# A two-layer hybrid encoder on one core: the first products in step over x, shorter lags for the last heads' norm, the FFN's sum of squares behind the second pair

## The chip, the cores and the metric

The kernel runs on one core of a Trainium2 chip. The metric is the device time of one execution in microseconds (us): the median of several runs. A profiled execution gives the trace; its span runs from the first to the last instruction.

## What is computed

A batch of one sequence: x is 512 tokens of 1024 channels, float32. Two layers, each of this form (shortened):

```python
h = rmsnorm(x, norm1_g[l])
u = h @ w_in[l]                       # q, k, v (512 each), GLU input (1024), Fourier input (512)
y_a = (rmsnorm(diff_attention(q, k, v, lam), subln_g[l]) * (1 - lam_init)) @ w_proj_a[l]
g = ga * sigmoid(gb)
cv = layernorm(depthwise_conv31(g, conv_w[l]) + conv_b[l])
y_b = silu(cv) @ w_proj_b[l]
y_c = real(fft2(four_in)) @ w_proj_c[l]
ga, gb, gc = split(sigmoid(h @ w_gate[l] + b_gate[l]))
x = x + (ga * y_a + gb * y_b + gc * y_c) @ w_out[l]
h2 = rmsnorm(x, norm2_g[l])
f_gate, f_up = split(h2 @ w_ffn_in[l])
x = x + (silu(f_gate) * f_up) @ w_ffn_out[l]
```

The attention has 8 heads of two 32-wide components. The FFN is 2816 wide.

## The kernel before

Everything lies with channels on the 128 partitions and the 512 tokens along a row, so x is 8 tiles of 128x512. Every product of float32 matrices is made of three matmuls (`gemm`): both sides are split into a high part (a cast on ACT) and a low part (a subtraction on VectorE, DVE), and high x high, high x low and low x high are summed in a PSUM bank. A weight chunk is 8 tiles of 128x128 for one output tile, 512 KB: `chunk` loads it on SyncE's queue (tile `wr`), casts it on ACT (`wh`, L202) and subtracts on DVE (`wl`, L203). x itself is split into tiles A and B (L158, L159); the normed x is split into X.

PSUM has 8 banks: three "main", two "s", two "att" and one "oth". A product that wants a bank of a tag waits until an earlier content of that tag is read.

The stages of a layer: `glu` makes four pairs of gated tiles from x that is not normed yet and scales the results by the inverse root of the mean square (`inv_rms`: squares on ACT, L386; added on GpSimd, L389; summed over partitions by a matmul with ones, L396; then L397 to L403 on DVE and ACT). In layer 1 the squares of all eight tiles are needed at the second gated pair. Then come q, k, v, the heads, the Fourier branch, the convolution, the gates and the projections of the three branches, `w_out`, and the FFN.

The attention (`heads`) and the convolution (`conv`: its taps on DVE, and at its end a norm over channels with two ones matmuls, L1112 and L1114 behind it) are pieces of work that are put among the products of the other stages. Each is an event with a due time (`later`), and `gemm` runs due events between its steps. `norm(hp)` sums the squares of a pair of heads and works out a scale on DVE, `scale(hp)` spreads it, transposes it and multiplies (L932); then `gemm_two` projects the heads. Their lags are `LAG_N` and `LAG_S`.

The FFN's input product is made in pairs, one gate tile and one up tile each, in a form with seven products of halves in place of eight (`pair_weights`, `pair_gemm`, L317, matmuls of 256 columns). The weights' combinations are made on DVE (L289 to L300) with casts on ACT. Pair u uses both banks of the tag ("s", "att", "main")[u % 3]; so the fourth pair needs the banks of the first. The first pair goes over all but the last of x's combined pieces first, and the last is added at its end, since it comes late. Each pair is evacuated by `unit` (L562 to L571), which needs the norm of this stage, `rb2`. It is asked for between the second pair's matmuls and the first pair's evacuation in the code:

```python
if done + j == 1:
    rb2 = self.inv_rms(acc, D, "ar", "rb")
while held:
    act.append(unit(*held.pop(0)))
```

The order on each engine is not that of the code. A scheduler sorts the instructions by a priority (`at`, in time units of the intended schedule) as their inputs become ready in a simulated timeline; each engine then runs its own queue in that fixed order. `after(ins)` ties an instruction behind the last matmul for the scheduler's order alone.

Of the kernel before, what the change touches and what calls it, by code (L numbers as in the profile page):

```python
# [16 lines left out]
P = 128  # L17
L = 2
D = 1024
# [15 lines left out]
WARM = 12  # L35
# [9 lines left out]
XP = (-100000, -15000, -15000, -15000, -10000, -10000, -10000, -10000)  # L45
SQP = 3000
# [9 lines left out]
LAG_S = 20000  # L56
LN = (6000, 14000, 29000)
# [23 lines left out]
def lam_init(l):  # L81
    return 0.8 - 0.6 * math.exp(-0.3 * l)
# [7 lines left out]
class Hybrid:  # L90
# [292 lines left out]
    def sq_add(self, x, acc, tag):  # L383
        nc = self.nc
        sq = self.slot(tag)
        nc.scalar.activation(sq, x, AF.Square)  # L386
# [19 lines left out]
    def build(self):  # L406
        nc, tc = self.nc, self.tc
        a = self.a
        with (
# [9 lines left out]
            self.params = [cp.tile([P, NCOL], F32, tag=f"par{l}", name=f"par{l}") for l in range(L)]  # L419
            nc.sync.dma_start(self.params[0], a["par"][0])  # L420
            self.x = []
            for m in range(KT):
                self.at(XP[m])
                xt = self.slot("V")
                nc.sync.dma_start(xt, a["xT"][m])
                self.x.append(xt)
# [9 lines left out]
            nc.gpsimd.dma_start(self.params[1], a["par"][1])  # L436
            self.ident = cp.tile([P, P], F32, tag="ident", name="ident")
            nc.gpsimd.dma_start(self.ident, a["ident"])
# [6 lines left out]
            self.rope = cp.tile([P, 2, NT, 8], F32, tag="rope", name="rope")  # L445
            nc.gpsimd.dma_start(self.rope, a["rope"])
            self.alt = cp.tile([P, 258], F32, tag="alt", name="alt")
            nc.gpsimd.dma_start(self.alt, a["alt"])
            self.c128f = cp.tile([P, P], F32, tag="c128f", name="c128f")
            nc.gpsimd.dma_start(self.c128f, a["dft"][0][:, 0:P])  # L450
            alt2 = cp.tile([P, 2], F32, tag="alt2f", name="alt2f")
            nc.gpsimd.dma_start(alt2, a["alt2"])
            self.alt2 = cp.tile([P, 2], F32R, tag="alt2", name="alt2")
            nc.vector.tensor_copy(self.alt2, alt2)
            self.xin = [a["xT"][m] for m in range(KT)]
            self.at(0)
            self.xg, self.acc = [], None
            for m in range(KT):
                self.next_x(0, m, self.x[m])
# [9 lines left out]
    def next_x(self, l, m, x):  # L469
        self.xg.append(self.split_to(x, "A", "B", self.par(l, "g1")[:, m : m + 1]))  # L470
        if l == 0:
            self.at(SQP)
        self.acc = self.sq_add(x, self.acc, "M")
        self.at(self.t)
# [9 lines left out]
    def tables(self):  # L484
        nc = self.nc
        self.dfts = []
# [13 lines left out]
    def main(self, l):  # L500
        nc = self.nc
        sm = self.small
        hb = sm(24, "hb")
        nc.vector.tensor_scalar_mul(hb, self.par(l, "bg"), 0.5)
        hcw = sm(4 * CW, "hcw")
        nc.vector.tensor_scalar_mul(hcw, self.par(l, "cw"), 0.5)
        self.hb, self.hcw = hb, hcw
# [70 lines left out]
        for rnd, nj in enumerate(ROUNDS):  # L578
# [3 lines left out]
            for j in range(nj):  # L582
# [4 lines left out]
                if done + j == 1:  # L587
                    rb2 = self.inv_rms(acc, D, "ar", "rb")
# [55 lines left out]

    def glu(self, l):
# [74 lines left out]
    def qk_post(self, l, which, banks):  # L720
# [43 lines left out]
        nc.vector.tensor_scalar_mul(  # L764
            gc, self.par(l, "gkc" if which else "gqc"), 1.0 if which else DC ** -0.5
        )
# [37 lines left out]
    def heads(self, l, t0, span):  # L804
# [5 lines left out]
        for i, (u, v) in enumerate((("lq1", "lk1"), ("lq2", "lk2"))):  # L810
            nc.vector.tensor_tensor(out=pr, in0=self.par(l, u), in1=self.par(l, v), op=ALU.mult)
# [7 lines left out]
        nc.vector.tensor_scalar_mul(sg, self.par(l, "sg"), 1.0 - lam_init(l))  # L819
# [38 lines left out]
        for u in range(NH * NT):  # L858
# [401 lines left out]
```

## Time and profile before

| what | value |
|---|---|
| median of 3 runs | 1625.96 us (1625.27 to 1627.03) |
| profiled execution, time | 1625.3 us |
| its span | 1623.5 us |
| TensorE (PE) busy | 1594.3 us, 98% of the span |
| VectorE (DVE) busy | 1354.2 us, 83% |
| ScalarE (ACT) busy | 833.1 us, 51% |
| GpSimd (POOL) busy | 164.6 us, 10% |
| mean granted clock of PE | 0.992 of full |
| DMA | 201.86 MB, 124 GB/s over the span |

An engine's busy time is the time with at least one of its instructions under way. The granted clock is the share of PE's full clock that it was given; 0.50 is its lower level, 1.2 GHz, and 1.00 is 2.4 GHz. Times in the trace count from the span's start. An idle time stands in square brackets behind the row that follows it, with what ended it.

### The profile page before, as it was taken

To read this page: it belongs to the slowest core of one execution; us is meant where nothing else is said; L and a number is where in the kernel's file an instruction comes from. 1 tells how busy PE (TensorE), PEld (TensorE's weight loads), DVE (VectorE), ACT (ScalarE), POOL (GpSimd) and SP (SyncE) were. 2 spreads that over 40 slices of the span, in tenths; PEclk is the share of its full clock that TensorE was granted. 3 is DMA by queue.
4 is the path that set the end of the run, shared out by engine and by line. 5 is a ranking of instruction groups with operands and counts; after the bars stand their busy time and mean duration, and the time that the engine had idled before them with its cause. 6 is when DMAs were issued, how large, how long until landed. Compare 5 with 4: busy or idle time off the path is not lost.

```text
span 1623.5 us, 24362 instructions
## 1 busy us (share of the span) xinstructions
PE 1594.3 (98%) x9108; PEld 1393.6 (86%) x9108; DVE 1354.2 (83%) x2419; ACT 833.1 (51%) x1377; POOL 164.6 (10%) x129
## 2 busy tenths in 40 slices
PE   8999999999989999999999999999999899999999
PEld 6888888887879898998988888887788898989998
DVE  7999999897888786858779999997968878878684
ACT  5445555674466363545443455556635654546351
POOL 4000000112430000000110000001033300000000
PEclk8999999999999999999999999999999999999999
DMA  5545233322445563636432542332225545546361
GB/s 194 181 139 170 79 108 101 104 77 82 147 113 138 160 139 110 163 111 182 118 119 88 174 148 76 103 111 86 72 84 152 145 113 151 136 130 156 88 159 65
DMA packets 74278, 201.86 MB, mean 124 GB/s; under 512 B 10400, under 2 KB 11552, under 8 KB 74160
## 3 DMA queue, kind: packets, MB, share of 16 engines
q1 hardware_dynamic: 67392, 176.11, 34.7%
q0 software_dynamic: 6768, 24.20, 8.9%
q8 instruction: 72, 1.18, 0.3%
q14 instruction: 46, 0.38, 0.1%
HBM read 186.37 MB, written 13.89 MB: 123 GB/s over the span
## 4 chain that ended last, share of the span: by engine, by line
PE 90%; DVE 5%; ACT 2%; issue 2%; DMA 1%; POOL 1%; SPq 0%; DVEq 0%; ACTq 0%; POOLq 0%
PE main L122 51%; PE s L317 9%; PE main L317 9%; PE att L317 8%; PE s L122 4%; PE att L122 3%; PE oth L122 3%; PE att L132 2%; POOL M L389 1%; DVE wl L203 1%; DMA V<-in_xT 0%; DMA wr<-in_w 0%; PE att L773 0%; DVE V L550 0%; DVE X L156 0%
## 5 line engine op out<-in xcount | busy, mean ns | idle before, releaser
L202 ACT CAST wh<-wr 128x1024 fp32r<-128x1024 f32 x180 | 188.2, 1050 | 248.4 <-PE main L122 112.5
L122 PE MATMUL main<-X,wh 128*128 128x512 f32 x864 | 277.7, 395 | 0.0
L203 DVE TENSOR_TENSOR wl<-wr,wh 128x1024 fp32r<-128x1024 f32 x180 | 232.7, 1293 | 40.9 <-ACT wh L202 40.0
L122 PEld LDWEIGHTS main<-X,wh 128*128 128x128 f32 x864 | 161.6, 189 | 32.8 <-issue 0.5
L1057 DVE SCALAR_TENSOR_TENSOR cv<-cv,hcw,cv 128x497 f32<-128x497 f32 (+14 forms) x240 | 176.3, 735 | 1.2
L122 PE MATMUL main<-X,wl 128*128 128x512 f32 x432 | 170.9, 396 | 0.0
L122 PE MATMUL main<-act,wh 128*128 128x512 f32 (+1 forms) x520 | 161.8, 391 | 0.0
L881 ACT ACTIVATE at<-s,mx 128x512 f32<-128x512 f32 x128 | 88.2, 689 | 56.3 <-DVE mx L879 49.8
L122 PEld LDWEIGHTS main<-act,wh 128*128 128x128 f32 x520 | 96.2, 188 | 21.6 <-DVE M L599 0.6
L122 PE MATMUL main<-A,wh 128*128 128x512 f32 x320 | 106.4, 391 | 0.0
L122 PE MATMUL main<-att,wh 128*128 128x512 f32 x320 | 100.1, 393 | 1.5 <-ACT att L155 1.5
L122 PE MATMUL main<-act,wl 128*128 128x512 f32 (+1 forms) x260 | 101.4, 391 | 0.0
L122 PE MATMUL main<-wh,X 128*128 128x512 f32 x288 | 96.7, 391 | 0.0
L122 PEld LDWEIGHTS main<-X,wl 128*128 128x128 f32 x432 | 81.6, 189 | 17.0 <-issue 0.5
L288 POOL DMA_DIRECT2D wlo<-in_w x44 | 38.3, 870 | 569.8 <-DVE V L600 164.6
L879 DVE TENSOR_REDUCE mx<-s 128x1 f32<-128x512 f32 x128 | 86.6, 680 | 3.8 <-PE s L122 3.1
L122 PE MATMUL main<-cv,wh 128*128 128x512 f32 x240 | 77.6, 394 | 2.6 <-ACT cv L155 2.5
L122 PE MATMUL main<-A,wl 128*128 128x512 f32 x192 | 74.7, 392 | 0.0
L122 PEld LDWEIGHTS main<-att,wh 128*128 128x128 f32 x320 | 59.7, 188 | 15.4 <-ACT att L155 1.7
L122 PEld LDWEIGHTS main<-A,wh 128*128 128x128 f32 x320 | 59.9, 188 | 12.5 <-issue 0.2
L122 PEld LDWEIGHTS main<-wh,X 128*128 128x128 f32 x288 | 54.0, 188 | 11.0
L389 POOL TENSOR_TENSOR M<-M,M 128x512 f32<-128x512 f32 x28 | 52.4, 1870 | 103.6 <-ACT M L386 61.4
(356 smaller groups left out, 4117.1 us busy)
## 6 DMA issues: line engine op xcount, KB each, us to landing
wr<-in_w SPq DMA_DIRECT2D x224, 512.0 KB, 3.6
wlo<-in_w POOLq DMA_DIRECT2D x44, 512.0 KB, 5.5
cv<-in_w SPq DMA_DIRECT2D x80, 256.0 KB, 4.7
dqk<-at SPq DMA_DIRECT2D x32, 256.0 KB, 4.0
qst<-dqk SPq DMA_DIRECT2D x96, 64.0 KB, 2.0
kst<-dqk SPq DMA_DIRECT2D x96, 64.0 KB, 1.9
V<-in_xT SPq DMA_DIRECT2D x8, 256.0 KB, 8.0
att<-dftd SPq DMA_DIRECT2D x8, 256.0 KB, 4.0
```

Of the source, the lines that this page charges most:

```text
L122: return self.pin(self.nc.tensor.matmul(out, lhsT=lhsT, rhs=rhs, start=start, stop=stop))
L132: self.pin(self.nc.tensor.transpose(ps[:, s], src[:, s], self.ident))
L202: nc.scalar.copy(hi, raw)
L203: nc.vector.tensor_tensor(out=lo, in0=raw, in1=hi.bitcast(F32), op=ALU.subtract)
L288: nc.gpsimd.dma_start(l2, src2, accum_op=ALU.add)
L317: self.nc.tensor.matmul(ps, lhsT=a[:, s], rhs=b, start=start and k == ks[0] and i == 0, stop=last and i == 2, skip_group_check=True,)
L389: nc.gpsimd.tensor_tensor(out=sq, in0=acc, in1=sq, op=ALU.add)
L879: nc.vector.tensor_reduce(out=mx, in_=ps, axis=AX.X, op=ALU.max, negate=True)
L881: nc.scalar.activation(e, ps, AF.Exp, bias=mx, accum_out=z1 if c else z0)
L1057: ins = nc.vector.scalar_tensor_tensor(out=acc[:, a:b], in0=g[:, a + d : b + d], scalar=w[:, t : t + 1], in1=acc[:, a:b], op0=ALU.mult, op ...
```

## The change

Three things are edited.

1. The start of layer 1. The loads of x and of the first two weight chunks follow a list, `FIRST`: each of the two chunks comes in halves, the first halves through ACT's queue, and a small load brings the eight columns of the norm's gain ahead of the other parameters. Splits are made in the same order. The first gated pair takes its matmuls in turns for each tile of x (`gemm_first`) in place of all tiles for one output and then for the other. The squares' sums move from GpSimd to DVE, and squares, sums and several small scalings are tied behind matmuls; the ones matmul comes behind the second pair. The constants' loads move from the start into `tables`, behind the gated pairs. There are 10 warm-up matmuls in place of 12.
2. The last pair of heads takes the lags `LAST` in place of `LAG_N` and `LAG_S`, in both layers.
3. The FFN's ones matmul is tied behind the second pair's matmuls, in both layers.

The core of the diff:

```diff
-WARM = 12
+WARM = 10
-XP = (-100000, -15000, -15000, -15000, -10000, -10000, -10000, -10000)
-SQP = 3000
+FIRST = (
+    ("x", 0, "sync"), ("w", 0, 0, "scalar"), ("x", 1, "sync"), ("w", 1, 0, "scalar"), ("x", 2, "sync"),
+    ("x", 3, "sync"), ("w", 0, 1, "sync"), ("w", 1, 1, "sync"), ("x", 4, "sync"), ("x", 5, "sync"),
+    ("x", 6, "sync"), ("x", 7, "sync"),
+)
 LAG_N = 5000
 LAG_S = 20000
+LAST = (2500, 8000)
...
+    def gemm_first(self, *tags):
+        banks = [self.bank(tag) for tag in tags]
+        self.wi += len(tags) * CHUNK
+        for k, (xh, xl) in enumerate(self.xg):
+            s = slice(k * P, (k + 1) * P)
+            for ps, (hi, lo) in zip(banks, self.first):
+                self.at(self.t)
+                self.mm(ps, hi[:, s], xh, k == 0, False)
+                self.mm(ps, hi[:, s], xl, False, False)
+                self.lastmm = self.mm(ps, lo[:, s], xh, False, k == KT - 1)
+                self.t += 3 * PASS
+        self.at(self.t)
+        return banks
...
-        nc.gpsimd.tensor_tensor(out=sq, in0=acc, in1=sq, op=ALU.add)
+        (engine or nc.gpsimd).tensor_tensor(out=sq, in0=acc, in1=sq, op=ALU.add)
...
-    def inv_rms(self, acc, n, tag, out):
+    def inv_rms(self, acc, n, tag, out, behind=False):
-        self.mm(ps, self.ones, acc, True, True)
+        ins = self.mm(ps, self.ones, acc, True, True)
+        if behind:
+            self.after(ins)
...
+            for n, (kind, i, *rest) in enumerate(FIRST):
+                self.at(-100000 + n)
+                queue = getattr(nc, rest[-1])
+                if kind == "x":
+                    queue.dma_start(self.x[i], a["xT"][i])
+                else:
+                    o = slice(rest[0] * T, (rest[0] + 1) * T)
+                    queue.dma_start(raws[i][:, o], a["w"][0, i][:, o])
...
-                    rb2 = self.inv_rms(acc, D, "ar", "rb")
+                    rb2 = self.inv_rms(acc, D, "ar", "rb", True)
...
-            pa = self.gemm(self.xg, GB[2 * j])
-            if j == 1:
-                rb = self.inv_rms(self.acc, D, "M", "rb")
-            pb = self.gemm(self.xg, GB[2 * j + 1])
+            if l == 0 and j == 0:
+                pa, pb = self.gemm_first(GB[0], GB[1])
+                for x in self.x:
+                    self.acc = self.sq_add(x, self.acc, "M", nc.vector)
+            else:
+                pa = self.gemm(self.xg, GB[2 * j])
+                if j == 1 and l > 0:
+                    rb = self.inv_rms(self.acc, D, "M", "rb")
+                pb = self.gemm(self.xg, GB[2 * j + 1])
+                if j == 1 and l == 0:
+                    rb = self.inv_rms(self.acc, D, "M", "rb")
+            if j == 0:
+                self.scales(l)
...
-                self.later(t + LAG_T + LAG_V + LAG_N, "att", lambda hp=u // 8: norm(hp))
-                self.later(t + LAG_T + LAG_V + LAG_N + LAG_S, "att", lambda hp=u // 8: scale(hp))
+                dn, ds = (LAG_N, LAG_S) if u < NH * NT - 1 else LAST
+                self.later(t + LAG_T + LAG_V + dn, "att", lambda hp=u // 8: norm(hp))
+                self.later(t + LAG_T + LAG_V + dn + ds, "att", lambda hp=u // 8: scale(hp))
```

Since the scheduler fills the queues anew, instructions move at other places too. Three places follow, each before and after; a row is an instruction with its line, output and inputs. The changed kernel's lines are 4 higher in the helpers (`mm`, L122, is its L126) and up to 53 higher behind them, and its tile numbers 6 higher.

PE at the FFN's ones matmul of layer 1, before. `s` and `att` are the banks of the first and second pair; B and X are parts of x, whi, wlo, qst and A of the weights:

```order
L317 MATMUL att_4857<-B_4594,whi_4827 128x256
L317 MATMUL att_4857<-B_4595,whi_4827 128x256
L317 MATMUL att_4857<-B_4594,wlo_4828 128x256
L122 MATMUL oth_4945<-M_4675,ones 128x512
L317 MATMUL s_4728<-B_4689,qst_4713 128x256
L317 MATMUL att_4856<-B_4689,A_4839 128x256
L317 MATMUL s_4729<-B_4693,whi_4703 128x256
```
PE where the ones matmul stands in the changed kernel, at the end of the second pair; `main` is the third pair's bank:

```order
L335 MATMUL att_4863<-B_4600,wlo_4836 128x256
L335 MATMUL att_4863<-B_4699,whi_4835 128x256
L335 MATMUL att_4863<-B_4700,whi_4835 128x256
L335 MATMUL att_4863<-B_4699,wlo_4836 128x256
L126 MATMUL oth_4951<-M_4681,ones 128x512
L335 MATMUL main_5016<-at_4391,whi_4991 128x256 x2
L335 MATMUL main_5016<-at_4391,wlo_4992 128x256
```
The ones matmul moved from the head of the first pair's rest to the end of the second pair.

DVE behind the same ones matmul, before, up to the reads of the first pair's banks (`s_4728`, `s_4729`); `ar` and `rb` are the norm's steps, cv, wr and kst combinations of weights:

```order
L156 TENSOR_TENSOR A_5147<-cv_5119,A_5146 128x512
L402 SCALAR_TENSOR_TENSOR ar_4947<-ar_4951,ar_4947 128x512
L156 TENSOR_TENSOR kst_5007<-cv_4983,qst_5006 128x512
L403 SCALAR_TENSOR_TENSOR rb_4949<-ar_4947,rb_4949 128x512
L289 TENSOR_TENSOR cv_5255<-wr_5251,wr_5253 128x512
L562 TENSOR_TENSOR M_4955<-s_4728,rb_4949 128x256
L563 TENSOR_TENSOR M_4955<-s_4728,M_4778 128x256
L567 TENSOR_TENSOR M_4960<-s_4729,M_4778 128x256
```
DVE there in the changed kernel, where the banks are `s_4734` and `s_4735`, read in the last three rows:

```order
L419 TENSOR_SCALAR ar_4953<-oth_4951 128x512
L307 TENSOR_TENSOR cv_5398<-cv_5390,cv_5394 128x512
L424 SCALAR_TENSOR_TENSOR ar_4953<-ar_4957,ar_4953 128x512
L160 TENSOR_TENSOR kst_5274<-cv_5261,qst_5273 128x512
L308 TENSOR_TENSOR cv_5390<-cv_5392,cv_5390 128x512
L425 SCALAR_TENSOR_TENSOR rb_4955<-ar_4953,rb_4955 128x512
L160 TENSOR_TENSOR A_5413<-cv_5398,A_5412 128x512
L318 TENSOR_TENSOR cv_5261<-wr_5259,cv_5262 128x512
L309 TENSOR_TENSOR cv_5399<-cv_5394,cv_5390 128x512
L598 TENSOR_TENSOR M_4961<-s_4734,rb_4955 128x256
L599 TENSOR_TENSOR M_4961<-s_4734,M_4784 128x256
L603 TENSOR_TENSOR M_4966<-s_4735,M_4784 128x256
```
The ones matmul's result now comes behind the preparation of the fifth pair; the rows between L419 and the reads include L307 of the changed kernel (L289 of before) with the combination that the sixth pair begins with.

PE ahead of the first matmul on cv (the convolution's normed output) in layer 1, before; `main_3708` and `main_3789` are gates, `att_3270` a transposed piece of attention:

```order
L122 MATMUL main_3708<-X_368,wh_3711 128x512
L122 MATMUL main_3708<-X_367,wl_3712 128x512
L122 MATMUL main_3708<-X_372,wh_3711 128x512
L122 MATMUL main_3708<-X_373,wh_3711 128x512
L122 MATMUL main_3708<-X_372,wl_3712 128x512
L132 MATMUL att_3270<-ident,at_3190 128x128 x4
L122 MATMUL main_3761<-cv_2835,wh_3764 128x512
L122 MATMUL main_3789<-X_337,wh_3764 128x512
```
PE there in the changed kernel, from a score on; `att_3508` is a product of attention weights and values:

```order
L126 MATMUL s_3520<-kst_3398,qst_3394 128x512
L136 MATMUL att_3482<-ident,at_3370 128x128 x4
L126 MATMUL att_3508<-wth_3333,V_1260 128x256
L126 MATMUL att_3508<-wtl_3334,V_1260 128x256
L126 MATMUL att_3508<-wth_3333,V_1266 128x256
L126 MATMUL att_3508<-wtl_3334,V_1266 128x256
L126 MATMUL att_3508<-wth_3333,V_1272 128x256
L126 MATMUL att_3508<-wtl_3334,V_1272 128x256
L126 MATMUL att_3508<-wth_3333,V_1278 128x256
L126 MATMUL att_3508<-wtl_3334,V_1278 128x256
L126 MATMUL s_3526<-kst_3406,qst_3402 128x512
L126 MATMUL main_3767<-cv_2841,wh_3770 128x512
L126 MATMUL main_3795<-X_330,wh_3770 128x512
```
The gates' matmuls on X stood ahead of cv before; in the changed kernel attention pieces do, and the matmuls on X follow.

## Rows read from the trace of the kernel before

**Rows 1.** the chain that ended last, shares by engine (part 4 of the page)
```profile
PE 90%; DVE 5%; ACT 2%; issue 2%; DMA 1%; POOL 1%; SPq 0%; DVEq 0%; ACTq 0%; POOLq 0%
```

**Rows 2.** waits of PE by releaser: us in total, times, longest
```profile
PE oth L122 <- POOL M L389: 9.1, 2, 4.5
PE s L122 <- ACT wh L202: 3.7, 1, 3.7
```

**Rows 3.** the start: timeline (start, us, instruction, idle before), windows 0-10 and 10-12
```profile
4.11 0.72 ACT L158 ACTIVATE A<-V,par 128x512 fp32r<-128x512 f32 x1 [1.87 <-DMA V<-in_xT]
8.71 1.04 ACT L202 CAST wh<-wr 128x1024 fp32r<-128x1024 f32 x1 [3.27 <-DMA wr<-in_w]
...
27.27 1.23 DVE L203 TENSOR_TENSOR wl<-wr,wh 128x1024 fp32r<-128x1024 f32 x1 [0.26 <-ACT wh L202]
...
19.62 0.39 PE L122 MATMUL s<-B,wh 128*128 128x512 f32 x1
26.66 0.39 PE L122 MATMUL main<-A,wh 128*128 128x512 f32 x1
...
11.08 12.38 POOL L389 TENSOR_TENSOR M<-M,M 128x512 f32<-128x512 f32 x7 [6.39 <-ACT M L386]
...
0.00:10.00 10.00, 5.23 (x25) 5.05 (x26) 3.49 (x27) 4.11 (x8) 3.61 (x10) 0.95 0.80 259
10.00:12.00 2.00, 1.96 (x4) 1.01 (x5) 2.00 (x4) 2.00 (x4) 0.92 (x1) 0.50 1.03 402
```

**Rows 4.** the end of layer 1's convolution, timeline of PE
```profile
314.03 1.02 PE L122 MATMUL oth<-cv,ones 128*128 128x512 f32 x2
330.10 0.50 PE L122 MATMUL main<-cv,wh 128*128 128x512 f32 x1
```

**Rows 5.** layer 2's convolution's end: timeline (PE, ACT) and a window
```profile
1123.24 1.02 PE L122 MATMUL oth<-cv,ones 128*128 128x512 f32 x2
1138.84 0.79 PE L122 MATMUL main<-cv,wh 128*128 128x512 f32 x1 [2.55 <-ACT cv L155]
...
1130.70 1.04 ACT L202 CAST wh<-wr 128x1024 fp32r<-128x1024 f32 x1
...
1132.00:1142.00 10.00, 6.64 (x21) 4.95 (x20) 9.04 (x19) 9.25 (x15) 0.00 (x0) 0.50 0.30 92
```

**Rows 6.** the last heads of layer 1, timeline of PE
```profile
400.61 0.66 PE L132 MATMUL oth<-ident,at 128*128 128x128 f32 x4 [0.26 <-ACT at L189]
402.76 1.22 PE L122 MATMUL main<-att,wh 128*128 128x512 f32 x4 [1.49 <-ACT att L155]
```

**Rows 7.** the FFN's ones matmul, layer 1: timeline (PE, DVE) and a window
```profile
476.28 1.83 PE L122 MATMUL oth<-M,ones 128*128 128x512 f32 x2 [4.54 <-POOL M L389]
477.12 1.20 PE L317 MATMUL s<-B,qst 128*128 128x256 f32 x1
482.04 0.40 PE L317 MATMUL s<-X,whi 128*128 128x256 f32 x2
...
473.22 1.28 DVE L156 TENSOR_TENSOR B<-ts,B 128x512 fp32r<-128x512 f32 x2
...
477.00:480.00 3.00, 3.00 (x12) 2.43 (x11) 0.82 (x2) 0.76 (x2) 0.00 (x0) 0.50 0.00 0
```

**Rows 8.** "s" banks in the FFN of layer 1, line 289 in layer 2
```profile
490.68 0.28 PE L317 MATMUL main<-at,whi 128*128 128x256 f32 x1
496.44 0.28 PE L317 MATMUL s<-at,whi 128*128 128x256 f32 x1
...
483.38 1.28 ACT L399 ACT_TABLE_LOAD   x1
...
491.20 0.41 DVE L567 TENSOR_TENSOR M<-s,M 128x256 f32<-128x256 f32 x1
498.55 0.69 DVE L289 TENSOR_TENSOR cv<-cv,cv 128x512 f32<-128x512 f32 x1 [1.61 <-DMA cv<-in_w]
...
1302.47 0.69 DVE L289 TENSOR_TENSOR cv<-cv,cv 128x512 f32<-128x512 f32 x1 [0.40 <-DMA cv<-in_w]
```

More of the change, by code (lines that the diff above doesn't have):

```diff
@@ L381, in par, with sq_add @@
         return self.params[l][:, lo:hi]
[L383 removed]
+    def sq_add(self, x, acc, tag, engine=None):
         nc = self.nc
         sq = self.slot(tag)
[L386 removed]
+        ins = nc.scalar.activation(sq, x, AF.Square)
+        if engine is not None:
+            self.after(ins)
         if acc is None:
             return sq
[L389 removed]
+        (engine or nc.gpsimd).tensor_tensor(out=sq, in0=acc, in1=sq, op=ALU.add)
         return sq
[L392 removed]
+    def inv_rms(self, acc, n, tag, out, behind=False):
         nc = self.nc
         ps = self.bank("oth")
[L395 removed]
+        ins = self.mm(ps, self.ones, acc, True, True)
+        if behind:
+            self.after(ins)
         m = self.slot(tag)
@@ L419, in build @@
             self.params = [cp.tile([P, NCOL], F32, tag=f"par{l}", name=f"par{l}") for l in range(L)]
-            nc.sync.dma_start(self.params[0], a["par"][0])
[L421 to L426, printed above, removed]
+            g1 = cp.tile([P, KT], F32, tag="g1first", name="g1first")
+            nc.scalar.dma_start(g1, a["par"][0][:, 0:KT])
+            self.x = [self.slot("V") for _ in range(KT)]
+            raws, his, los = (
+                [
+                    self.wp.tile([P, CHUNK * P], dt, tag=tag, name=self.nm("w" + tag), bufs=WB[i])
+                    for _ in range(2)
+                ]
+                for i, (tag, dt) in enumerate((("raw", F32), ("hi", F32R), ("lo", F32R)))
+            )
+            for n, (kind, i, *rest) in enumerate(FIRST):
[6 more added lines that the diff above has]
+                    queue.dma_start(raws[i][:, o], a["w"][0, i][:, o])
+            self.at(-90000)
+            nc.sync.dma_start(self.params[0], a["par"][0])
             self.at(-50000)
@@ L444, in build @@
             nc.vector.memset(self.blk[64:128, 1:2], 1.0)
[L445 to L454, printed above, removed]
-            self.xin = [a["xT"][m] for m in range(KT)]
+            self.cp = cp
+            self.xin = [a["xT"][m] for m in range(KT)]
+            self.xg, self.acc = [None] * KT, None
+            for n, (kind, i, *rest) in enumerate(FIRST):
+                self.at(-40000 + n)
+                if kind == "x":
+                    self.xg[i] = self.split_to(self.x[i], "A", "B", g1[:, i : i + 1])
+                else:
+                    o = slice(rest[0] * T, (rest[0] + 1) * T)
+                    self.split(raws[i][:, o], his[i][:, o], los[i][:, o])
+            self.first = list(zip(his, los))
             self.at(0)
-            self.xg, self.acc = [], None
-            for m in range(KT):
-                self.next_x(0, m, self.x[m])
             self.events = []
@@ L485, in tables, with load @@
         nc = self.nc
+        cp, a = self.cp, self.a
+        def load(name, shape, src):
+            t = cp.tile(list(shape), F32, tag=name, name=name)
+            self.after(nc.gpsimd.dma_start(t, src))
+            return t
+        self.rope = load("rope", (P, 2, NT, 8), a["rope"])
+        self.ident = load("ident", (P, P), a["ident"])
+        self.alt = load("alt", (P, 258), a["alt"])
+        self.c128f = load("c128f", (P, P), a["dft"][0][:, 0:P])
+        alt2 = load("alt2f", (P, 2), a["alt2"])
+        self.alt2 = cp.tile([P, 2], F32R, tag="alt2", name="alt2")
+        nc.vector.tensor_copy(self.alt2, alt2)
+        self.after(nc.gpsimd.dma_start(self.params[1], a["par"][1]))
         self.dfts = []
@@ L643, in merge, with scales @@
             nc.gpsimd.tensor_tensor(out=t, in0=t, in1=th, op=ALU.add)
+    def scales(self, l):
+        nc = self.nc
+        self.hb = self.small(24, "hb")
+        self.after(nc.vector.tensor_scalar_mul(self.hb, self.par(l, "bg"), 0.5))
+        self.hcw = self.small(4 * CW, "hcw")
+        self.after(nc.vector.tensor_scalar_mul(self.hcw, self.par(l, "cw"), 0.5))
     def glu(self, l):
@@ L763, in qk_post @@
         gc = self.small(1, f"gc{which}")
-        nc.vector.tensor_scalar_mul(
+        self.after(nc.vector.tensor_scalar_mul(
             gc, self.par(l, "gkc" if which else "gqc"), 1.0 if which else DC ** -0.5
-        )
+        ))
         out = []
@@ L810, in heads @@
         for i, (u, v) in enumerate((("lq1", "lk1"), ("lq2", "lk2"))):
-            nc.vector.tensor_tensor(out=pr, in0=self.par(l, u), in1=self.par(l, v), op=ALU.mult)
+            self.after(nc.vector.tensor_tensor(out=pr, in0=self.par(l, u), in1=self.par(l, v), op=ALU.mult))
             nc.vector.tensor_reduce(out=sl[:, i : i + 1], in_=pr, axis=AX.X, op=ALU.add)
@@ L818, in heads @@
         sg = self.small(1, "sgc")
-        nc.vector.tensor_scalar_mul(sg, self.par(l, "sg"), 1.0 - lam_init(l))
+        self.after(nc.vector.tensor_scalar_mul(sg, self.par(l, "sg"), 1.0 - lam_init(l)))
         self.at(self.t)
```

12 lines of the change are left out of this document (1 added, 11 removed).

## The prediction

> **What bounds the kernel now.** I read the chain that ended last first: PE holds 90% of it [rows 1], so a microsecond counts only where PE's queue stands still or runs at its lower clock. The waits of PE say where that is [rows 2]: at the top are the two sums of squares of the FFN's norm behind GpSimd (9.1 us in two waits) and the first weight cast (3.7). Both stand at places that the change edits. So I went to the stretches of the edits one by one, and to the order of the instructions for what stands there now. In each stretch the reader should look for the start of a PE row and for what ended the idle time before it.
>
> The profiled execution took 1625.3 us, of which the span is 1623.5. The median of the runs is 1625.96, 0.66 above it. The sum below is made against 1625.3. Less than 0.2% (3.25 us) can't be told from no change here.
>
> **The start.** Before, x and whole chunks of 512 KB are under way together: A of the first x tile is split at 4.11, but the first cast of weights only comes at 8.71, after 3.27 us of waiting for its load [rows 3]. By then PE's clock is at the lower of its two levels: 0.50 in 10 to 12 us [rows 3], so 1.2 GHz. From 19.62 on the matmuls follow each other in (26.66 - 19.62) / 31 = 0.227 us, and the 48 of the first pair are through at 26.66 [rows 3].
>
> After the change the same 48 take turns over x (PE's order). The bytes they need are 8 x 256 KB of x and 4 x 256 KB of weights, 3.1 MB. At 259 GB/s over the first 10 us and 402 behind it [rows 3] these are in at 11.3. Each x tile costs ACT 0.72 [rows 3], each half chunk some 0.6 (half of a cast of 1.04 us [rows 3] and its fixed part): 8 x 0.72 + 4 x 0.6 = 8.2 us from 4.1 on, which is 12.3, and the last lo part is there at about 13.5. So neither sets the end; PE does. First matmul: two tiles' A and a half cast behind 4.1, about 6.0; 48 x 0.227 = 10.9; end 16.9, 9.8 earlier. The next pair's casts stand behind four squares on ACT; I put 0.6 on it. The term is **-9.2**. If PE starts at half clock and has full speed only 6 us later, 3 us are lost: -6.2. With the casts hidden: -10.
>
> The squares' seven adds move from GpSimd, where they take 12.38 us [rows 3], to VectorE, at some 0.64 each (a lo part of twice the columns takes 1.23 [rows 3]). That is 4.5 us more for VectorE, hidden under the matmuls of the next pairs, whose outputs it can't scale before the norm anyway; without that cover it would be up to 4.5. The constants' loads on GpSimd's queue and the small scalings go behind the first pair; their users, rotary tables and transposes, come tens of microseconds later: nothing. Two warm-up matmuls less lie in an idle stretch of PE: nothing.
>
> The first half chunks go through ACT's queue, and the rows say that the transfers are what is waited for, at 259 GB/s over the first 10 us [rows 3]. The Trainium skill, DMA: Bandwidth & Descriptors, section "Issuing engines are not separate DMA queues", says that transfers from all issuing engines run on the same 16 DMA engines and interleave, and that a second issuer saves only issue time. By that rule x would slow the first halves as it slowed the first chunk, and the start would give about -6 in place of -9.2.
>
> **The convolution's end, layer 1.** PE's queue is filled anew, and one place gets worse. Between the second ones matmul of the convolution's norm (314.03) and the first matmul on cv (330.10) PE had 16.1 us of other work [rows 4], mostly gate matmuls on X. Now there stand 5 scores, 12 transposes, 16 half-width matmuls and four blk columns, and the X matmuls come only behind cv: 5 x 0.227 + 12 x 0.09 + 16 x 0.12 + 0.4 = 4.5 us, with 0.86 for ones 5.4. What the chain from ones to cv takes when little hides it, layer 2 of before shows: 1123.24 to 1138.84, 15.6 us [rows 5]. A cast of a weight chunk (1.04) stands in that one on ACT [rows 5] and not in the new one; I take 14.5. PE waits 14.5 - 5.4 = 9.1. In layer 2 the clock was 0.50 from 1132 to 1142 [rows 5], 3.2 us of it behind the wait, worth 1.6. Term **+10.7**. The bounds are 0, if cv's chain runs as far ahead as before, and +12 if it takes its 15.6.
>
> **The convolution's end, layer 2.** The same place gets better: X matmuls and attention pieces of some 9.0 us stand between, where there were 6.3 of the kind. Term **-2.7** (0 to -5).
>
> **The last heads.** PE waits 0.26 for the transposes and 1.49 for the cast behind them [rows 6]. With the shorter lags 44 matmuls of the projection (10 us) stand between the sums and the transposes, where there were 16, and 25 (5.7 us) behind them, against a last step of 402.76 - 400.61 = 2.2. Term **-1.75**; layer 2 has no such wait, 0. A loss is excluded by what fills the gap: matmuls on the earlier heads.
>
> **The FFN's norm.** Before, PE stands 4.54 us at the ones matmul (476.28), whose add on GpSimd is late; the clock falls (0.50 in 477 to 480), and 27 half-width matmuls behind it take from 477.12 to 482.04 [rows 7]. With ones behind the second pair these 27 wait only for the last lo part of x, written from 473.22 to 474.50 [rows 7]. From 473.9 on they take 27 x 0.12 = 3.2 (0.12 is (496.44 - 490.68) / 48 [rows 8]): 477.1. That is 4.9 gained; ones itself (477.12 - 476.28 = 0.84) is paid later: **-4.1** a layer.
>
> But the norm's result comes 14 us later, and the fourth pair needs it: it uses the two "s" banks, which the evacuation of the first pair frees. Before, that was done at 491.61 and PE came at 496.44 [rows 8], 4.8 us of slack. Now PE is at the fourth pair 0.84 + 5.76 = 6.6 us after the end of the second. In that time ACT must get to a table load (1.28 [rows 8]) and two activations, 3.7 us with ones, and VectorE's queue then holds seven instructions of 0.6 and two reads of the bank: 3.7 + 4.2 + 0.7 = 8.6, so PE waits at least 2.0. And the row ahead of these seven is line 289 of the kernel before (cv from cv, cv), which needs a weight load of the sixth pair. Everything on VectorE behind it, lines 402, 403 and 562 too, is then held. Before, it waited for that load until 498.55, 7.9 us after the second pair's end [rows 8], and until 1302.47 in layer 2 [rows 8]. At 7.9 the banks are free 0.6 + 4.2 + 0.7 = 5.5 later, at 13.4: PE waits 6.8. The load's issue moves forward with PE, but the transfers are busy; I take the load between the ends, at 5.7 and 4.9: waits of 4.6 and 3.8. A wait of 4.5 dropped the clock for some 3.5 us [rows 7], worth 1.75; I count it whole in layer 1 and half in layer 2. Terms: -4.1 + 4.6 + 1.75 = **+2.25** and -4.1 + 3.8 + 0.9 = **+0.6**. Bounds: -2.1 and +4.45 each.
>
> **Sum.** -9.2 + 10.7 - 2.7 - 1.75 + 2.25 + 0.6 = -0.1: 1625.2 by the profiled run, 1625.9 by the median. I say 1625.5: a gain at the start, given back at the convolution's end.
>
> **The rivals.**
> - Faster, by the FFN: the load is there early, the banks are free after 8.6, and the clock holds. Both layers give -2.1 instead of +2.85 in all, 7 less: 1618.5. For it: the load is issued earlier when PE is. Against: it was waited for in both layers.
> - Faster, by the convolution: queue and chain overlap more, half the wait (4.5) and no fall of the clock: 6.2 less, 1619.3. For it: layer 1 hid all of its chain before. Against: layer 2 of before, where nearly the same order waited.
> - Slower, by the load: VectorE stands at line 289 as long as before, +4.45 a layer, 6 more than I count: 1631.5. It decides where the load lands 7 us or more behind the second pair.
> - The start does not do what it says: the first halves come as late as the chunk did, and the clock is low: -6.2, 1628.5. The row for it is the 3.27 us that the first cast waited. The skill's rule on issuing engines would end here too.
>
> **The numbers.** My case (within 3.25 of no change) has 0.35; faster by the FFN 0.17, by the convolution 0.20; slower by the load 0.16; the start, with a part of that wait, 0.12. So faster 0.37, same 0.35, slower 0.28. Both faster cases together reach 1612, both slower ones 1634.5; 1614 to 1634 leaves out some 2 in 10. The likeliest case alone is 1622 to 1629.
>
> **What would show it.** The first pair through near 17 us at a clock of 1.00; a wait of PE of 8 to 10 us ahead of cv in layer 1; none for the last heads; none for GpSimd at ones, but one of 2 to 7 us at the fourth pair's first matmul into "s", ended by VectorE. I am wrong if there is no such wait at the fourth pair or none ahead of cv, or if VectorE, with 4.5 us more at the start, comes late somewhere in the convolution.

## The result and the profile after

The changed kernel takes 1638.96 us in the median (1638.34 to 1640.64, four runs) against 1626.03 for the kernel before beside it: a ratio of 1.008 [1.0067, 1.0093]. It is slower, and lies above the predicted range. The profiled execution took 1640.64 us, 15.3 more than that of before.

The page after, span, engines and the shares of the chain that ended last:

```profile
span 1638.9 us, 24380 instructions
PE 1599.7 (98%) x9104; PEld 1398.2 (85%) x9104; DVE 1351.0 (82%) x2428; ACT 835.4 (51%) x1379; POOL 153.8 (9%) x122
PE 86%; DVE 8%; ACT 2%; DMA 2%; issue 2%; ACTq 0%; DVEq 0%
```

The work on PE is the same but for two warm-up matmuls, and the chain runs over DVE for 8% of the span where it was 5% [rows 1]. Waits of PE after, by releaser (us in total, times, longest):

```profile
PE s L335 <- DVE M L599: 13.0, 2, 6.5
PE main L126 <- ACT cv L159: 6.6, 2, 5.3
PE s L126 <- ACT at L934: 4.1, 6, 1.4
PE oth L126 <- ACT cv L421: 2.4, 1, 2.4
```

The wait for GpSimd [rows 2] is gone, and a longer one for DVE stands at the top: the fourth FFN pair's banks, once a layer.

Where the time went is read by taking the start of the same PE matmul in both traces, after minus before. PE is 7.4 us ahead behind the start, 6.3 late when layer 1's branches are projected, 11.4 late behind the fourth FFN pair, 11.8 late at 800 to 900 us, 10.7 behind layer 2's branches and 15.6 behind its FFN. So layer 1's branches cost 13.7, the two FFNs 5.1 and 4.9, layer 2's branches give 1.1. Traces of one and the same order differ by up to 3 us in such numbers, as the single edits below show.

**The start.** Timeline of PE and ACT (start, us, instruction, idle before) and a window:

```profile
1.09 4.63 PE L126 MATMUL oth<-ones 128*128 128x128 f32 x20 [1.09 <-DVE blk L474]
6.78 0.50 PE L126 MATMUL s<-A,whi 128*128 128x512 f32 x1 [1.06 <-ACT whi L159]
9.60 0.50 PE L126 MATMUL s<-A,whi 128*128 128x512 f32 x1 [0.51 <-ACT whi L159]
19.28 0.39 PE L126 MATMUL main<-A,wh 128*128 128x512 f32 x1
...
8.93 0.62 ACT L159 CAST whi<-wraw 128x512 fp32r<-128x512 f32 x1 [0.52 <-DMA wraw<-in_w]
...
6.00:8.00 2.00, 1.07 (x4) 0.59 (x5) 1.39 (x3) 1.04 (x3) 0.00 (x0) 1.00 0.99 330
```

The second pair begins at 19.28, where it was 26.66 [rows 3], at full clock throughout. Three of the four half casts wait for their loads, about half a microsecond each, and the first matmul on x comes at 6.78. With the first halves on ACT's queue the DMA moved 260 GB/s in the first 10 us; before it was 259 [rows 3].

**The convolution's end, layer 1.** Timeline of PE and a window that shows the clock (the number behind POOL's count):

```profile
324.79 1.02 PE L126 MATMUL oth<-cv,ones 128*128 128x512 f32 x2
330.20 1.84 PE L126 MATMUL oth<-blk,at 128*128 128x2 f32 x8 [2.37 <-ACT cv L421]
335.75 0.80 PE L126 MATMUL s<-kst,qst 96*128 96x512 f32 x1 [1.36 <-ACT at L934]
341.11 0.80 PE L126 MATMUL main<-cv,wh 128*128 128x512 f32 x1 [1.32 <-ACT cv L159]
...
330.00:345.00 15.00, 11.63 (x36) 8.91 (x37) 10.60 (x27) 13.10 (x23) 0.00 (x0) 0.51 0.12 31
```

From ones to cv it is 16.3 us, as in [rows 4] (16.1), but PE has little to do in it: it stands idle for 5.5 us, and falls to its lower clock, which lasts until 347 us, 6 us behind the first matmul on cv. The ones matmul itself comes 10.8 later than before [rows 4], although the start is 7.4 earlier. That was not predicted.

**The FFN.** Timeline of layer 1, by engine, and a window:

```profile
487.99 5.68 SPq L282 DMA_DIRECT2D cv<-in_w  x4
...
491.98 1.02 PE L126 MATMUL oth<-M,ones 128*128 128x512 f32 x2
505.18 0.77 PE L335 MATMUL s<-at,whi 128*128 128x256 f32 x2 [6.44 <-DVE M L599]
...
495.64 0.69 DVE L419 TENSOR_SCALAR ar<-oth 128x512 f32<-128x512 f32 x1
499.46 0.69 DVE L307 TENSOR_TENSOR cv<-cv,cv 128x512 f32<-128x512 f32 x1 [3.14 <-DMA cv<-in_w]
500.07 0.68 DVE L424 SCALAR_TENSOR_TENSOR ar<-ar,ar 128x512 f32<-128x512 f32 x1
501.88 0.68 DVE L425 SCALAR_TENSOR_TENSOR rb<-ar,rb 128x512 f32<-128x512 f32 x1
504.29 0.42 DVE L598 TENSOR_TENSOR M<-s,rb 128x256 f32<-128x256 f32 x1
504.95 0.41 DVE L603 TENSOR_TENSOR M<-s,M 128x256 f32<-128x256 f32 x1
...
505.00:512.00 7.00, 6.82 (x35) 6.85 (x36) 6.02 (x15) 4.06 (x6) 0.00 (x0) 0.56 0.36 66
```

DVE stands 3.14 us at L307 for the sixth pair's load, which SP's queue began to issue only 4 us before the second pair's end (the ones matmul's start). The norm's rows L424 and L425 stand behind it, and the reads that free the banks behind those. Layer 2 repeats it (the same two rows of its timeline):

```profile
1308.97 0.69 DVE L307 TENSOR_TENSOR cv<-cv,cv 128x512 f32<-128x512 f32 x1 [3.13 <-DMA cv<-in_w]
1314.69 0.77 PE L335 MATMUL s<-at,whi 128*128 128x256 f32 x2 [6.53 <-DVE M L599]
```

### The profile page after: what moved, and what is told of

It is laid out like the page before. It is cut to its first block, busy times and chain, and to the rows that moved or that the text cites. A ratio compares the mean times of both kernels' runs of the same rounds, so it can differ in the third digit from the quotient of the medians.

```text
span 1638.9 us, 24380 instructions
## 1 busy us (share of the span) xinstructions
PE 1599.7 (98%) x9104; PEld 1398.2 (85%) x9104; DVE 1351.0 (82%) x2428; ACT 835.4 (51%) x1379; POOL 153.8 (9%) x122
## 4 chain that ended last, share of the span: by engine, by line
PE 86%; DVE 8%; ACT 2%; DMA 2%; issue 2%; ACTq 0%; DVEq 0%
PE main L126 50%; PE s L335 9%; PE att L335 8%; PE main L335 8%; PE s L126 3%; PE att L126 3%; PE oth L126 3%; PE att L136 1%; DMA cv<-in_w 1%; DVE wl L207 1%; DVE cv L1110 1%; DVE mx L932 0%; DVE A L160 0%; DVE B L160 0%; DMA wr<-in_w 0%
## 5 line engine op out<-in xcount | busy, mean ns | idle before, releaser
L126 PE MATMUL main<-X,wh 128*128 128x512 f32 x864 | 281.1, 398 | 0.7 <-DVE M L1061 0.7
L207 DVE TENSOR_TENSOR wl<-wr,wh 128x1024 fp32r<-128x1024 f32 x178 | 228.2, 1283 | 45.1 <-ACT wh L206 44.6
L126 PEld LDWEIGHTS main<-X,wh 128*128 128x128 f32 x864 | 163.5, 191 | 34.3 <-DVE M L1061 0.7
L126 PE MATMUL main<-X,wl 128*128 128x512 f32 x432 | 171.5, 397 | 0.0
L126 PE MATMUL main<-act,wh 128*128 128x512 f32 (+1 forms) x520 | 161.8, 391 | 0.0
L126 PEld LDWEIGHTS main<-act,wh 128*128 128x128 f32 x520 | 96.2, 188 | 21.6 <-DVE M L635 0.6
L126 PE MATMUL main<-A,wh 128*128 128x512 f32 x320 | 106.2, 391 | 0.0
L126 PE MATMUL main<-act,wl 128*128 128x512 f32 (+1 forms) x260 | 101.4, 391 | 0.0
L126 PE MATMUL main<-att,wh 128*128 128x512 f32 x320 | 99.8, 392 | 0.0
L126 PEld LDWEIGHTS main<-X,wl 128*128 128x128 f32 x432 | 82.3, 191 | 17.3 <-issue 0.3
L126 PE MATMUL main<-wh,X 128*128 128x512 f32 x288 | 96.7, 391 | 0.0
L126 PE MATMUL main<-cv,wh 128*128 128x512 f32 x240 | 78.5, 395 | 6.6 <-ACT cv L159 6.6
L126 PE MATMUL main<-A,wl 128*128 128x512 f32 x192 | 74.3, 390 | 0.0
L126 PEld LDWEIGHTS main<-att,wh 128*128 128x128 f32 x320 | 59.8, 188 | 13.7 <-DVE A L678 0.6
L126 PEld LDWEIGHTS main<-A,wh 128*128 128x128 f32 x320 | 59.9, 188 | 12.2
L126 PEld LDWEIGHTS main<-wh,X 128*128 128x128 f32 x288 | 53.9, 188 | 11.0
L126 PE MATMUL main<-att,wl 128*128 128x512 f32 x160 | 62.7, 392 | 0.0
```

The lines of the kernel that those rows point to most:

```text
L126: return self.pin(self.nc.tensor.matmul(out, lhsT=lhsT, rhs=rhs, start=start, stop=stop))
L207: nc.vector.tensor_tensor(out=lo, in0=raw, in1=hi.bitcast(F32), op=ALU.subtract)
```

## The experiments

The theory behind the result had two halves: the tie costs what its new wait at the fourth pair costs, and the start's lead is lost in layer 1's branches because VectorE can't follow. The rivals were the shorter lags, the squares' adds that moved to VectorE, and the order of gates and attention pieces at the convolution's end.

**Each edit alone.** The third is taken out of the changed kernel in no_tie and start_only (first pair of lines), the second in start_only too (second pair); tie_only and last_only add one of them to the kernel before:

```diff
-rb2 = self.inv_rms(acc, D, "ar", "rb", True)
+rb2 = self.inv_rms(acc, D, "ar", "rb")
-LAST = (2500, 8000)
+LAST = (5000, 20000)
```

> The first edit alone (loads and first pair in step over x, sums of squares on VectorE, constants later). My theory: the wait of the attention and convolution of layer 1 comes from this edit, since PE's queue there is the one of the changed kernel; then PE is 7.4 us ahead up to 127 us and about 8 us behind after layer 1's branches (15.4 lost there), layer 2 gives back about 1, the FFN stages are as before: 1626 + 7 = 1633. Rival, that the losses come from the later edits reaching back through the scheduler: 1626 - 7.4 = 1618.6.

> The third edit alone on the kernel before. My theory: in each FFN 4.9 us are gained at the ones matmul and about 6.5 of waiting plus 3 of low clock are paid at the fourth pair's first matmul into s, because VectorE stands at the sixth pair's first combination until its load lands: +5 a layer, 1636. Rival, that the load is late only because the whole kernel is shifted by the other edits: waits of 2 us, -2 a layer, 1622.

> The second edit alone on the kernel before. My theory: the 1.75 us ahead of and behind the last heads' transposes in layer 1 go and nothing else changes: 1624.3, at the edge of what can be told. Rival, that the norm placed earlier holds up another instruction: no change or slower.

> The changed kernel without the third edit. My theory, parts that add up: 1639 - 10 = 1629 to 1631, slower than before by the convolution's end of layer 1 alone. Rival, that the parts share one cause (VectorE behind by the work it took over): 1636 or more, with a wait in the FFN all the same.

| kernel | median, us | ratio to before, 95% |
|---|---|---|
| start_only | 1635.91 | 1.0054 [1.0041, 1.0066] |
| tie_only | 1635.65 | 1.0054 [1.0041, 1.0068] |
| last_only | 1627.54 | 1.0003 [0.9994, 1.0012] |
| no_tie | 1634.22 | 1.0049 [1.0036, 1.0062] |

The first and the third edit each cost some 0.5%, and the second nothing. The order of instructions on all five engines is the same in last_only as before, and the same in no_tie as in start_only, so their times are two measurements of one program: the shorter lags move nothing here.

This also shows how far one trace can be trusted. In last_only and tie_only, which have the order of before up to the FFN, PE is 1.4 us ahead of the trace of before already behind the start; against them the start's gain is 6.0, not 7.4. The changed kernel, start_only and no_tie have one order up to the first FFN and lose 13.7, 12.5 and 10.8 in layer 1's branches; PE's clock over 330 to 345 us was 0.51, 0.54 and 0.77. The costs of the two edits don't add up: alone they cost 9 us each, together 13. The tie also changes the order in layer 2's branches; they give 1.1 in the changed kernel, and lose 2.2 in start_only and 1.9 in no_tie. In tie_only the wait at the fourth pair is there without the first edit (wait of PE; DVE's timeline):

```profile
PE s L317 <- DVE M L565: 12.0, 2, 7.0
...
492.45 0.69 DVE L289 TENSOR_TENSOR cv<-cv,cv 128x512 f32<-128x512 f32 x1 [3.61 <-DMA cv<-in_w]
```

In start_only PE is 7.4 us ahead behind the start and 5.1 late behind layer 1's branches, so that loss needs no tie. no_tie was expected at 1629 to 1631, on the belief that the parts add up, and that fell.

**Is it the load ahead of the norm?** tie_free_first is the changed kernel with the sixth pair's first combination ordered behind the first pair's release:

```diff
-        g(out=s1, in0=a21, in1=a22, op=ALU.add)
+        ins = g(out=s1, in0=a21, in1=a22, op=ALU.add)
+        if u == 5:
+            self.order(ins, self.release)
...
-            v(out=u[:, 0:h], in0=b2[:, h:T], in1=qw[:, 0:h], op=ALU.add)
+            ins = v(out=u[:, 0:h], in0=b2[:, h:T], in1=qw[:, 0:h], op=ALU.add)
+            if rnd == 0 and j == 0:
+                self.release = ins
```

> The changed kernel, with one thing more: VectorE's first combination for the sixth pair is tied behind the three reads that free the first pair's banks. My theory: VectorE waits for a weight load there, and the load is what keeps the banks. The wait at the fourth pair falls from 6.5 to about 1.5 us in each layer and the clock holds: 13 us less than the changed kernel, 1626, so that the third edit gains 3 to 4 a layer. Rival, that the chain from ones to the norm's result itself is too long (table load, two activations, other vector work): the wait stays over 4 us, 1634 or more.

It takes 1627.05 us, 1.0006 [0.9997, 1.0015] of before. Waits of PE and its timeline, then DVE's, and the fifth pair's second load (SP, L276) with its time to landing:

```profile
PE s L337 <- DVE M L601: 6.2, 2, 3.2
...
501.83 0.47 PE L337 MATMUL s<-at,whi 128*128 128x256 f32 x2 [3.23 <-DVE M L601]
...
493.16 0.69 DVE L307 TENSOR_TENSOR cv<-wr,wr 128x512 f32<-128x512 f32 x1 [4.74 <-issue]
496.42 0.68 DVE L421 TENSOR_SCALAR ar<-oth 128x512 f32<-128x512 f32 x1
499.73 0.68 DVE L427 SCALAR_TENSOR_TENSOR rb<-ar,rb 128x512 f32<-128x512 f32 x1
...
486.64 0.33 SPq L276 DMA_DIRECT2D wr<-in_w  x1
...
DMA to landing us min/median/max: 6.4/6.4/6.4
```

The wait falls from 6.5 to 3.2 (1.5 was expected): the load was half of it. Behind the other half stands the norm's own chain: the ones matmul starts at 491.83, but the norm's first row on DVE (L421) comes only at 496.42, behind five rows of the fifth pair's weights. The first of these has 4.74 us of idle time ahead of it for which the profile names no releaser. It starts 0.1 us behind the landing of that pair's second load (486.64 + 6.4 = 493.0); in the changed kernel the row and the landing are 492.38 and 492.3, in best 486.03 and 485.9. So the second half is most likely a load at the head of DVE's queue as well; no run tried it. The FFNs now cost 1.1 and 0.35 in place of 5.1 and 4.9. Of the rest of the gain some 3 us came in layer 2's branches, whose order moved too, so this kernel tells the wait, not the whole time.

**Is it cover at the convolution's end?** LEAD_B is the number of gate products on X that are made ahead of the products on cv. gates_ahead is no_tie with six in place of three, before_gates the kernel before with the same line, best is tie_free_first with it:

```diff
-LEAD_B = 3
+LEAD_B = 6
```

> The changed kernel without the third edit, and six gate products ahead of the convolution's end in place of three, so that 20 us of PE's work (layer 1) and 28 (layer 2) stand between the second ones matmul and the first matmul on cv, where there were 4.5 and 7.3. My theory: the chain from ones to cv takes 16 us whatever stands there, and only the lack of other work makes PE wait; waits and low clock there go in both layers, 12 and 8 us: 1616. Rival, that PE is then held by VectorE at another place, since VectorE is busy at 97% up to there: 1626 or more, with new waits in the gates or heads.

> The kernel before with six gate products ahead in place of three. Layer 1 had no wait there and layer 2 lost 8 to 10: 1617 by my theory, and the first edit, once covered, should then be worth its 7 us at the start beside it (this kernel against gates_ahead and best). Rival: no change, 1626, if the wait of layer 2 has another cause.

> The changed kernel with both remedies: the banks are freed first, and six gate products stand ahead. If both theories hold, the gains add up: 1639 - 13 - 20 = 1606, faster than either kernel by over 1%. If VectorE's backlog is the limit: 1615 to 1620.

gates_ahead takes 1620.09 us, 0.9964 [0.9951, 0.9976] of before; before_gates 1620.84, 0.997 [0.996, 0.998]; best 1622.24, 0.9979 [0.9971, 0.9988], far from its 1606 and behind gates_ahead, which has no tie. The windows of gates_ahead in the first heads and at the convolution's end, and then the same of the changed kernel:

```profile
150.00:190.00 40.00, 36.99 (x223) 31.56 (x222) 40.00 (x83) 21.53 (x45) 1.52 (x1) 1.00 0.29 87
300.00:345.00 45.00, 44.06 (x222) 36.09 (x220) 35.75 (x66) 33.93 (x59) 6.41 (x4) 1.00 0.31 92
```

```profile
150.00:190.00 40.00, 36.93 (x224) 31.47 (x223) 40.00 (x83) 21.39 (x45) 1.52 (x1) 1.00 0.29 87
300.00:345.00 45.00, 39.45 (x176) 31.27 (x175) 36.87 (x72) 34.05 (x62) 6.41 (x4) 0.84 0.30 84
```

With three more gate products on X there, PE is busy for 44.06 of 45 us at full clock, where it had 39.45 at 0.84. PE is then 0.5 ahead behind layer 1's branches, not 6.3 late (3.4 in no_tie). The ones matmul stands as late as in the changed kernel, at 325.56, so a late convolution costs PE time only where nothing covers it. But with the same cover the kernel before comes to the same time (its gain stands mostly in layer 2, about 4.5 us), so the first edit is worth some 1 us (1620.84 - 1620.09), which the intervals don't tell from nothing, and not 7.4. In best the wait at the fourth pair is 1.8 at most, and the FFNs give 1.2 and 1.0. With the cover, layer 1's branches still lose 6.7 us of the lead in gates_ahead and 6.8 in best, and nothing in before_gates.

**Is VectorE what is late?** fewer_taps is no_tie with 4 of the convolution's 31 taps less in layer 1 (16 instructions of 0.735, 11.8 us of VectorE); before_fewer_taps does that to the kernel before; pool_adds is no_tie with the squares' seven adds back on GpSimd (the last two lines).

```diff
+        if l == 0:
+            order = order[:-4]
...
-                    self.acc = self.sq_add(x, self.acc, "M", nc.vector)
+                    self.acc = self.sq_add(x, self.acc, "M")
```

> The first two edits (the changed kernel without the third), with 4 of the 31 taps of the convolution left out in layer 1: 16 instructions of 0.74, 11.8 us less for VectorE, nothing less for PE. My theory: VectorE's work, not PE's, sets the end of layer 1's branches, so that PE's lead of 7 us only makes it wait there. Then the wait ahead of cv goes and PE keeps most of the lead: 1635 - 13 = 1622. Rival, that the new order of PE's queue loses the time by itself: 1630 or more.

> The kernel before, with the same 4 taps left out in layer 1. My theory: without the lead PE does not wait for the convolution, so 11.8 us less of VectorE's work are worth nothing: 1626. Rival, that VectorE holds PE back in many small waits there: 1620 or less.

> The first two edits, with the seven adds of the squares back on GpSimd. If the 4.5 us that VectorE took over were what makes the convolution late, its end comes 4 to 5 us earlier and PE waits less: 1630. If they are a minor part (the attention's vector work, pulled ahead by PE's lead, being the larger): within 2 us of 1635, with the wait ahead of cv as it was.

fewer_taps takes 1625.89 us, 0.9998 [0.9989, 1.0006] of before; before_fewer_taps 1626.34, 1.0 [0.9991, 1.0008]; pool_adds 1633.23, 1.0043 [1.0029, 1.0056]. The same 11.8 us of VectorE are worth 8.3 to no_tie and nothing to the kernel before: only in the changed order does VectorE's work count. But more than VectorE's work changes, since the queues are filled anew: between the second ones matmul and the first on cv no matmul on X stands in no_tie, 94 stand in fewer_taps, and 46 stood before. So the 8.3 us are those of an earlier convolution and of the cover that came back with it. The taps' rows (min/median/max of one in ns, first and last start) of the kernels before, after and with fewer taps:

```profile
L1057 DVE SCALAR_TENSOR_TENSOR cv<-cv,hcw,cv x120: 716/735/752, 58.9 to 296.6; 128x497 f32<-128x497 f32 x8, 128x498 f32<-128x498 f32 x8, 128x499 f32<-128x499 f32 x8, 128x500 f32<-128x500 f32 x8
```

```profile
L1110 DVE SCALAR_TENSOR_TENSOR cv<-cv,hcw,cv x120: 710/735/753, 52.6 to 306.7; 128x497 f32<-128x497 f32 x8, 128x498 f32<-128x498 f32 x8, 128x499 f32<-128x499 f32 x8, 128x500 f32<-128x500 f32 x8
```

```profile
L1112 DVE SCALAR_TENSOR_TENSOR cv<-cv,hcw,cv x104: 717/735/750, 52.6 to 282.0; 128x501 f32<-128x501 f32 x8, 128x502 f32<-128x502 f32 x8, 128x503 f32<-128x503 f32 x8, 128x504 f32<-128x504 f32 x8
```

After, the taps begin 6 us earlier and end 10 later, at the same 735 ns each. The first tile takes 59.4 us in place of 42.0. What went ahead of the taps is mostly attention's vector work: 47 row maxima of scores (`mx`) start before the last tap ends, where it was 41, and with the rows that go with them (tiles at, wtl, ar and rt) attention has some 10 us more of VectorE by then. That the lead of PE brought them forward in the schedule is the likely reason; no run set it apart from the new order itself. The rows of the maxima up to the last tap's end, before and after:

```profile
L879 DVE TENSOR_REDUCE mx<-s x41: 659/678/693, 146.8 to 294.4; 128x1 f32<-128x512 f32 x41
```

```profile
L932 DVE TENSOR_REDUCE mx<-s x47: 629/681/692, 138.7 to 306.1; 128x1 f32<-128x512 f32 x47
```

From 60 to 300 us DVE (third number behind the length) is busy for 231.63 of 240 us after, 97%, and was for 232.91 before, so whatever goes ahead pushes taps behind:

```profile
60.00:300.00 240.00, 236.93 (x1186) 198.29 (x1186) 231.63 (x476) 124.54 (x233) 3.51 (x3) 1.00 0.42 125
```

The adds are not the cause: in pool_adds the last tap starts later still (311.5), with a lead of only 3.9 behind the start and the same 47 maxima ahead, and the wait ahead of cv stays.

**The norm's sum in another way.** vec_sum is gates_ahead (which has no tie) with the last of the FFN's square adds on VectorE. It was run since the tie removed a wait for that add at the price of another.

```diff
-        (engine or nc.gpsimd).tensor_tensor(out=sq, in0=acc, in1=sq, op=ALU.add)
+        (nc.vector if last else engine or nc.gpsimd).tensor_tensor(out=sq, in0=acc, in1=sq, op=ALU.add)
...
-                acc = self.sq_add(xt, acc, "M")
+                acc = self.sq_add(xt, acc, "M", last=m == KT - 1)
```

> The kernel with six gate products ahead and no tie, and the last add of the FFN's squares on VectorE in place of GpSimd, in both layers. It goes for the same wait as the third edit, but leaves ones where it was. My theory: the 4.5 us at ones are GpSimd's add of 6.1 us, VectorE needs 0.7; PE then waits only for the last parts of x, 1.4 us, and the clock holds; the banks are free as early as before. 4 to 5 us less a layer: 1611. Rival, that the squares or x itself are late: 1618 or more.

It takes 1610.69 us, 0.9905 [0.9892, 0.9919] of before: faster than both kernels, and as expected (1611). Its timeline (DVE, PE) and a window of PE, weight loads, DVE, ACT and POOL:

```profile
472.69 0.68 DVE L409 TENSOR_TENSOR M<-M,M 128x512 f32<-128x512 f32 x1
...
473.51 1.09 PE L126 MATMUL oth<-M,ones 128*128 128x512 f32 x2
475.00 0.39 PE L335 MATMUL s<-B,whi 128*128 128x256 f32 x1 [0.40 <-ACT B L159]
476.16 0.38 PE L335 MATMUL s<-B,qst 128*128 128x256 f32 x1 [0.65 <-DVE B L160]
...
470.00:477.00 7.00, 5.95 (x40) 4.82 (x40) 7.00 (x14) 3.83 (x7) 0.00 (x0) 1.00 0.01 2
```

The ones matmul stands at the place in PE's queue where it stood before [rows 7], without its wait, so the norm is early enough: PE has no wait for DVE at the fourth pair. Against before, the FFNs gain 4.5 and 3.7.

## Why the prediction was wrong

The sum came out 15.4 us too low by the profiled runs: 1.8 at the start, 4.8 in layer 1's branches, 1.6 in layer 2's, and 7.2 in the two FFNs.

- **The bound** was read rightly: PE's waits and low clock set the time.
- **The start**, -9.2, measured -7.4: the mechanism was right, the size was off. The casts waited 0.5 to 0.7 for halves that I had counted as there, and the first matmul came at 6.78, not at 6.0. The rival (-6.2, at low clock) did not come: the clock held. The rule of the Trainium skill that was weighed there (DMA: Bandwidth & Descriptors, "Issuing engines are not separate DMA queues") is borne out in direction only: the transfers still bind the casts, at the same rate as before, but the casts wait 0.5 to 0.7 us and not 3.27.
- **The convolution's end, layer 1**, +10.7. Place and kind were right, with two terms too small: the chain from ones to cv takes 16.3, not the 14.5 that I chose below [rows 5], and the lower clock lasted 6 us behind the first matmul on cv, worth 3, not 1.6. (In no_tie, with the same order, it rose before that matmul.) What PE had to do there, put at 5.4, took 10.8, most of it at the lower clock; with 5.5 of idle time, in pieces of at most 2.37 and not in one wait of 9.1, that is the 16.3. The layer's branches lost 13.7 where this step and the lags together gave 8.95. Some 2 us of that stand in the first heads (3.1 us of PE idle in 150 to 190, 0.9 before), which no step named.
- **The convolution's end, layer 2**, -2.7, measured -1.1 for all of that layer's branches; the wait itself was not set apart from the rest.
- **The last heads**, -1.75. The wait did go, but not by the lags: start_only has the same order there as no_tie, and last_only the same as before. The order of the first edit removed it. I read the difference between the two orders as the effect of the edit nearest to it.
- **The FFN's norm.** -4.1 at ones was right (5.0 by the second pair's end). The wait behind it was put at 4.6 and 3.8, from a load "between the ends" at 5.7 and 4.9 us behind the second pair. That was a middle value with no row behind it. The row that waits for the load came at 7.5 and 7.6, past the point that the rival "slower, by the load" named: SP issues it 4.0 us ahead of the second pair's end, where it was 2.6, but the row came only 0.4 earlier. With 7.5 in my own sum the wait is 7.5 + 5.5 - 6.6 = 6.4; PE waited 6.44 and 6.53, so the rest of the chain was right. The clock was 0.56 over the 7 us behind the wait, in both layers, worth 3 where I counted 1.75 and 0.9. Terms: +5.1 and +4.9 for +2.25 and +0.6. tie_free_first shows that this load makes half of the wait, and that the least wait, which I put at 2.0, was 3.2.

**The steps that failed.** In size it is above all the FFN's load, taken "between the ends" at 5.7 and 4.9 us, which landed at 7.5 and 7.6 and took the clock along; then the convolution's end of layer 1. In kind it is the sum itself: it took the start's gain and the convolution's loss as two terms that don't touch each other, so that without the loss the gain would be kept. From 60 to 300 us VectorE is 97% busy, and the taps stand last in it; in the changed order more of attention's vector work stands ahead of them, so the convolution ends 10 us later although PE is ahead. Even where gate products cover its end, the first edit is worth some 1 us (gates_ahead against before_gates). The last sentence of the prediction named a late VectorE as what would make me wrong, for the 4.5 us of adds; the place was right and the reason not (pool_adds).

**Open**: with cover, layer 1's branches still lose about 7 us of the lead; the windows show some 5 of it (the first heads, and idle and clock behind 345 us), not the rest. Whether the fifth pair's load is what holds the norm in tie_free_first was not tried.

## What to carry to other kernels

An earlier start was worth next to nothing here, where a later stage was set by another engine that was already full: look at the windows of every engine up to the next wait, and find what covers that wait, before counting the lead. Moving a late instruction back in PE's queue moves its result back too: follow that result to whoever holds a buffer for it, and look for an instruction ahead of it, in the same in-order queue, that waits for a load. Here one add on an engine that did it in 0.68 us removed the same wait without moving the ones matmul.

## What the runs showed of the hardware

The add that PE waited for is slow where VectorE is busy beside it without a break. Of the kernel before, the same 128x512 add on GpSimd twice (timeline), with DVE's rows beside the first and the last of its rows beside the second:

```profile
463.33 1.46 POOL L389 TENSOR_TENSOR M<-M,M 128x512 f32<-128x512 f32 x1 [0.58 <-DVE cv L291]
470.09 6.13 POOL L389 TENSOR_TENSOR M<-M,M 128x512 f32<-128x512 f32 x1 [5.30 <-ACT M L386]
...
463.21 0.42 DVE L331 TENSOR_TENSOR ts<-us 128x256 f32<-128x256 f32 x1
463.55 1.52 DVE L156 TENSOR_TENSOR at<-us,at 128x256 fp32r<-128x256 f32 x1
...
474.43 0.68 DVE L300 TENSOR_TENSOR cv<-cv,cv 128x512 f32<-128x512 f32 x1
```

It takes 1.46 us, or 6.13 while VectorE runs two-input rows back to back until 475.11; and a VectorE subtraction of 256 columns that begins inside the short add takes 1.52, until 465.07, just behind the add's end at 464.79; another row of 256 columns (L331) takes 0.42. Layer 2 has the long add too (6.13). On VectorE the add takes 0.68 (vec_sum). The Trainium skill, SBUF — State Buffer, section "SBUF: two separate sides", says that VectorE with two SBUF inputs and GpSimd share a port pair as an exclusive lock, and whoever comes second is blocked for the whole instruction. Both rows agree with it; no run here separated the port from other causes.
